# A transformer block's attention and projections written out in a fixed order on four engines

## Chip, cores and metric

One core of a Trainium2 chip runs the whole program. The time is what the device took for one execution, in microseconds. Three executions of the kernel before took 1728.81, 1731.15 and 1735.82 us; the median is 1731.15.

## What is computed

The program runs two transformer blocks on 256 tokens of 1024 features, in fp32. The change touches the first part of the first block only. Cut to that, the reference is:

```python
h = rmsnorm(x, norm1_g)
qa, ka, va, qb, kb, vb, ga, gb = split(h @ w_in)          # 1024 -> 4352
ya = neighbourhood_attention(qa, ka, va, rpb)             # 8 heads of 64, bias and window mask
qh = axial_rope(rmsnorm(qb, q_norm_g))                    # 8 heads
kh = axial_rope(rmsnorm(kb, k_norm_g))                    # 2 key/value heads, each for 4 query heads
yb = gqa_attention(qh, kh, vb)
merged = sigmoid(ga) * (ya @ w_proj_a) + sigmoid(gb) * (yb @ w_proj_b)
x = x + merged @ w_out
# then the first block's expert layer and the whole second block, which stay as they are
```

Both attentions are softmax(q k^T / 8 [+ bias and mask]) v over all 256 keys.

## The kernel before

`block1_mix` (L143) does this part. The normed input is turned to `hT`, split in two fp32r halves (hi and lo), so that a product of fp32 accuracy is three fp32r matmuls (`mm3`, L78 to L82). The input weights come as 34 blocks of 512 KB. A block is loaded by SP to a `raw` tile (four buffers), `split` (L65) makes `whi` on ScalarE (L66) and `wlo` on VectorE (L67), and there are four pairs of such tiles. With `stationary` a block is the stationary operand and 256 tokens stream: 24 matmuls of 256 columns. With `moving` a block streams past `hT`: 12 matmuls of 512 columns, or 24 of 256.

Eight blocks give the queries and keys of the first attention (`qk_block`, L175, copied to `qkT` by VectorE at L178), four its values `va`, four the queries and two the keys and values of the second attention, and sixteen the two gates (`gate`, L307, copied to `sg` by ScalarE at L310, the sigmoid later at L331). A pair of heads of the second attention goes through a norm and a rotation on VectorE (L261 to L303) before it can be scored.

`attention` (L198) does a pair of heads at a time, one head after the other:

```python
nc.tensor.matmul(pS[:, i], q_of(pair)[s, ...], k_of(pair)[s], start=True, stop=True)   # L205, 64 rows
# bias and maximum on VectorE (L212 to L218), exponential with its sum on ScalarE (L221)
# reciprocal and product on VectorE (L223, L225), four transposes (L229), copy on ScalarE (L231)
nc.tensor.matmul(pY[:, j], v_of(pair, kc), PT[j][:, kc], ...)                          # L236, 128 columns
# the head's 64 rows of pY are split into yT (hi on ScalarE, lo on VectorE)
```

The sums with V use the values of both heads as weights (128 columns) and keep the 64 rows of one. A matmul with fp32 operands (scores and sums) stands as two records in the trace; a transpose stands as one.

The order of the work is set in two ways. Where `manual_schedule` is open for an engine, its instructions stand in the order of the code. Otherwise the planner of the framework orders each engine's instructions by its own costs and priorities. Before the change only SP is in code order in `block1_mix`, and only up to the last constant (L153 to L251); TensorE, VectorE and ScalarE are the planner's. The gates are written between the pairs, two to a pair, and the planner moves them. After the gates come the four sigmoids and the products with `w_proj`, `w_out`, whose loads and splits (`load_w`, L70) the planner places too. Later parts of the program (L845, L1278) have stretches in code order on all engines.

Of the kernel before, what the change touches and what calls it, by code (L numbers as in the profile page):

```python
# [142 lines left out]
def block1_mix(e, a, x, begin):  # L143
# [7 lines left out]

    warm(e, AF.Sqrt, e.eps)
    man = tc.manual_schedule(engines={mybir.EngineType.SP})  # L153
    man.__enter__()
    for t in range(2):
        nc.sync.dma_start(x[t], a["x"][t * P:(t + 1) * P])
        if t == 0:
            g1 = row(e, pool, a["norm1_g"], D, "g1", tag="g1", eng=nc.sync)
    hT = [keep.tile([P, NC8, T], F32R, tag=f"hT{i}", name=f"hT{i}") for i in range(2)]
    for tt in range(2):  # L160
        h = wk.tile([P, D], F32, tag="h", name=f"h{tt}")
        norm_rows(e, wk, x[tt], g1, h)
        transposed(e, h, tt, hT[0], hT[1])
# [3 lines left out]
    load = wide_load(e, [(e.stage, e.raw_bufs)], [(e.stage, e.w_bufs), (pool, 2)])  # L167

    def stationary(blk, out, eng=None):
        wh, wl = load(a["w_in_a"][blk], eng=eng)  # L170
        wh, wl = (w.rearrange("p (c n) -> p c n", c=NC8) for w in (wh, wl))
        for c in range(NC8):
            mm3(e, out, wh[:, c], wl[:, c], hT[0][:, c], hT[1][:, c], c == 0, c == NC8 - 1)

    def qk_block(b):  # L175
        p = ps.tile([P, 512], F32, tag="mm", name=uid(e, "pqk"), bufs=e.mm_bufs)
        stationary(b, p[:, :T])
        nc.vector.tensor_copy(qkT[:, b], p[:, :T])  # L178

    def moving(blks, width, per):  # L180

        pt = [ps.tile([P, 512], F32, tag="mm", name=uid(e, "pmv"), bufs=e.mm_bufs) for _ in range(2)]
        for i, b in enumerate(blks):
# [12 lines left out]
    yT = [[keep.tile([P, 4, T], F32R, name=f"yT{s}{i}") for i in range(2)] for s in "ab"]  # L196

    def attention(pair, q_of, k_of, v_of, bias_of, dst):  # L198

        PT = []  # L200
        for j in range(2):
            s = slice(j * 64, (j + 1) * 64)
            pS = ps.tile([P, 2, T], F32, tag="att", name=uid(e, "pS"), bufs=e.att_bufs)
            for i, tt in enumerate((1, 0)):
                nc.tensor.matmul(pS[:, i], q_of(pair)[s, tt * P:(tt + 1) * P], k_of(pair)[s], start=True, stop=True)  # L205
            S = wk.tile([P, 2, T], F32, tag="S", name=uid(e, "S"), bufs=2)
            mx = wk.tile([P, 2], F32, tag="mx", name=uid(e, "mx"), bufs=3)
            sm = wk.tile([P, 2], F32, tag="sm", name=uid(e, "sm"), bufs=3)
            if bias_of is not None:
                b = bias_of(2 * pair + j)  # L210
# [12 lines left out]
            nc.vector.reciprocal(sm, sm)  # L223
# [20 lines left out]
    nc.sync.dma_start(bias.rearrange("p a b c -> p (a b c)"), a["na_win"])
    mask = pool.tile([P, 64], F32, name="mask")
    nc.sync.dma_start(mask, a["na_mask"])
    rope = pool.tile([P, 2, 2, 64], F32, name="rope")
    nc.sync.dma_start(rope.rearrange("p a b c -> p (a b c)"), a["rope"])
    gqk = [row(e, pool, a["gqa_q_norm_g"], 64, "gq", eng=nc.sync), row(e, pool, a["gqa_k_norm_g"], 64, "gk", eng=nc.sync)]

    man.__exit__(None, None, None)  # L251
    for b in (2, 6, 3, 7):
        qk_block(b)
    for tt, p in enumerate(moving(range(0, 4), 512, 2)):
        nc.vector.tensor_copy(va[:, tt], p)

    pq = moving(range(4, 8), 512, 2)
    pkv = moving(range(8, 10), 256, 4)
    qT = pool.tile([P, 4, T], F32, name="qT")
    kT = pool.tile([P, 2, T], F32, name="kT")  # L260
    ss = wk.tile([P, 2, 10], F32, tag="ss", name="ss", bufs=1)  # L261
    qks = []
    for tt in range(2):
        qk = wk.tile([P, 10, 64], F32, tag="qk", name=uid(e, "qk"))
        qks.append(qk)
        nc.scalar.activation(qk[:, :8].rearrange("p a b -> p (a b)"), pq[tt], AF.Copy)
        nc.scalar.activation(qk[:, 8:].rearrange("p a b -> p (a b)"), pkv[tt][:, :128], AF.Copy)
        for d in range(2):
            nc.scalar.activation(vb[:, tt, :, d], pkv[tt][:, 128:256].rearrange("p (a b) -> p a b", a=2), AF.Copy)
        sq = wk.tile([P, 10, 64], F32, tag="sq", name=uid(e, "sq"))  # L270
        nc.vector.tensor_mul(sq, qk, qk)
        nc.vector.tensor_reduce(ss[:, tt], sq, axis=AX.X, op=OP.add)
    rqk = rstd(e, wk, ss.rearrange("p a b -> p (a b)"), 20, 1.0 / 64, "gqr")
    for tt, qk in enumerate(qks):
        r = rqk[:, tt * 10:(tt + 1) * 10]
# [13 lines left out]
        nc.vector.tensor_tensor(qk, qk, rope[:, tt, 0][:, None, :].to_broadcast([P, 10, 64]), op=OP.mult)  # L289
        kd = wk.tile([P, 2, 2, 64], F32, tag="kd", name=uid(e, "kd"))  # L290
# [3 lines left out]
        qf = qk.rearrange("p h n -> p (h n)")  # L294
        kf = kd.rearrange("p a b n -> p (a b n)")
# [9 lines left out]
    sg = keep.tile([P, 16, T], F32, name="sg")  # L305

    def gate(b):  # L307
        p = ps.tile([P, 512], F32, tag="mm", name=uid(e, "pg"), bufs=e.mm_bufs)
        stationary(8 + b, p[:, :T])
        nc.scalar.activation(sg[:, b], p[:, :T], AF.Copy)  # L310

    bv = bias.rearrange("p h v c -> p h (v c)")

    def masked(h):
        if h % 2 == 0:
            v = bias[:, h:h + 2].rearrange("p a b c -> p (a b) c")
            nc.vector.tensor_tensor(v, v, mask[:, None, :].to_broadcast([P, 12, 64]), op=OP.add)
        return bv[:, h]

    for pair in range(4):  # L320
        attention(pair, lambda q: qkT[:, q], lambda q: qkT[:, 4 + q],
                  lambda q, kc: va[:, kc, q * P:(q + 1) * P], masked, yT[0])
        for b in (2 * pair, 2 * pair + 1):
            gate(b)
    for pair in range(4):
        attention(pair, lambda q: qT[:, q], lambda q: kT[:, q // 2],
                  lambda q, kc: vb[:, kc, q // 2].rearrange("p a b -> p (a b)"), None, yT[1])
        for b in (8 + 2 * pair, 9 + 2 * pair):
            gate(b)
# [1730 lines left out]
```

## Time and profile before

| what | value |
|---|---|
| median of three executions | 1731.15 us |
| profiled execution | 1730.54 us |
| its span, first to last instruction | 1728.7 us |
| mean granted TensorE clock | 0.987 |
| TensorE busy in the span | 1643.9 us (95%) |
| VectorE busy | 1117.3 us (65%) |
| ScalarE busy | 745.1 us (43%) |
| first block's part that the change touches | about 14 to 160 us |

A row of a timeline gives the start, the duration, the engine (PE is TensorE, PEld its weight loads, DVE is VectorE, ACT is ScalarE, SP issues the loads), the line of the kernel, the operation, the tile written and those read, the shape, how many instructions were merged, and in brackets how long the engine stood idle before and whose end released it. Matmuls are pipelined: the distance of two starts tells what one costs, not its duration. An instruction's busy time includes what overlaps with its neighbour.

### The profile page before, as it was taken

How to read it: one execution, taken by the hardware profiler on the slowest of the kernel's cores; microseconds unless marked ns; L12 is line 12 of the kernel's file. 1: busy time of each engine (PE TensorE's matmuls, PEld its weight loads, DVE VectorE, ACT ScalarE, POOL GpSimd, SP SyncE). 2: the span in 40 equal slices, each digit the busy share in tenths (PEclk: the TensorE clock that was granted, in tenths of full speed). 3: DMA queues.
4: the chain of work that ended last, by engine and by line, in shares of the span. 5: the costliest groups of instructions: out<-in, count | busy, mean ns of one | idle time of the engine just before them, and what ended most of it. 6: DMA issues, size and time to landing. Idle time of an engine off the chain costs nothing.

```text
span 1728.7 us, 29531 instructions
## 1 busy us (share of the span) xinstructions
PE 1643.9 (95%) x11301; PEld 1292.7 (75%) x11301; DVE 1117.3 (65%) x2212; ACT 745.1 (43%) x1217; POOL 162.2 (9%) x84
## 2 busy tenths in 40 slices
PE   7999898999999999999899998998999999999996
PEld 7888798899989999787788876987875544444442
DVE  6765789994989999877777767689653111111113
ACT  4576444444544444444454455655542222222212
POOL 0000001232112122000000003024001000000000
PEclk9999999999999999999999999999999999999998
DMA  7442744456545555587888855442067799999994
GB/s 263 145 135 62 221 157 157 155 169 191 151 131 161 170 171 172 176 287 269 300 285 286 289 162 163 146 147 76 23 266 273 273 408 409 408 409 408 409 406 159
DMA packets 108118, 390.91 MB, mean 226 GB/s; under 512 B 12656, under 2 KB 12944, under 8 KB 107840
## 3 DMA queue, kind: packets, MB, share of 16 engines
q1 hardware_dynamic: 106128, 384.58, 63.7%
q0 software_dynamic: 976, 2.82, 0.6%
q8 instruction: 91, 1.49, 0.4%
q10 hardware_dynamic: 864, 1.53, 0.3%
q14 instruction: 59, 0.48, 0.1%
HBM read 386.79 MB, written 2.10 MB: 225 GB/s over the span
## 4 chain that ended last, share of the span: by engine, by line
PE 67%; DVE 17%; DMA 9%; issue 4%; ACT 3%; POOL 0%; DVEq 0%; SPq 0%; ACTq 0%
PE pgu L1572 10%; PE acc L696 8%; DMA raw<-in_w_ada 7%; PE py L1591 5%; PE pu L80 5%; PE pu L81 5%; PE pu L82 5%; DVE wlo L67 4%; PE pga L1757 3%; PE py L1854 3%; PE pg L642 2%; PE pmv L82 1%; PE pmv L80 1%; ACT whi L66 1%; PE pmv L81 1%
## 5 line engine op out<-in xcount | busy, mean ns | idle before, releaser
L66 ACT ACTIVATE whi<-raw 128x1024 fp32r<-128x1024 f32 x361 | 379.5, 1054 | 299.0 <-PE pu L81 138.5
L67 DVE TENSOR_TENSOR wlo<-raw,whi 128x1024 fp32r<-128x1024 f32 x315 | 385.2, 1226 | 81.3 <-ACT whi L66 80.3
L82 PE MATMUL pu<-pxT,wlo 128*128 128x256 f32 x1024 | 288.7, 282 | 11.6 <-DVE wlo L67 8.8
L80 PE MATMUL pu<-pxT,whi 128*128 128x256 f32 x1024 | 290.9, 284 | 0.7 <-ACT whi L66 0.7
L81 PE MATMUL pu<-pxT,whi 128*128 128x256 f32 x1024 | 287.5, 281 | 0.0
L696 PE MATMUL acc<-whi,hh 128*128 128x512 f32 x1008 | 279.6, 395 | 6.4 <-ACT hh L66 4.2
L696 PEld LDWEIGHTS acc<-whi,hh 128*128 128x128 f32 x1008 | 189.0, 189 | 51.3 <-DVE hh L67 5.2
L82 PEld LDWEIGHTS pu<-pxT,wlo 128*128 128x128 f32 x1024 | 194.0, 189 | 14.1 <-DVE wlo L67 10.9
L80 PEld LDWEIGHTS pu<-pxT,whi 128*128 128x128 f32 x1024 | 194.0, 189 | 0.9 <-ACT whi L66 0.9
L81 PEld LDWEIGHTS pu<-pxT,whi 128*128 128x128 f32 x1024 | 194.0, 189 | 0.0
L1572 PE MATMUL pgu<-raw,xg 128*32 128x512 f32 (+2 forms) x988 | 183.4, 597 | 0.0
L67 POOL TENSOR_TENSOR wlo<-raw,whi 128x1024 fp32r<-128x1024 f32 x46 | 128.1, 2788 | 499.6 <-ACT whi L66 498.1
L696 PE MATMUL acc<-wlo,hh 128*128 128x512 f32 x504 | 157.6, 393 | 2.2 <-DVE wlo L67 2.2
L66 ACT ACTIVATE hh<-H 128x256 fp32r<-128x256 f32 x126 | 52.6, 418 | 173.4 <-PE acc L696 171.6
L1572 PEld LDWEIGHTS pgu<-raw,xg 128*32 128x32 f32 (+2 forms) x988 | 52.4, 124 | 86.5 <-issue 74.9
L696 PEld LDWEIGHTS acc<-wlo,hh 128*128 128x128 f32 x504 | 94.8, 189 | 23.7 <-DVE wlo L67 3.8
L67 DVE TENSOR_TENSOR yl<-py,yh 128x512 fp32r<-128x512 f32 x50 | 34.6, 692 | 107.1 <-ACT yh L66 107.1
L1591 PE MATMUL py<-raw,th 128*32 128x512 f32 (+2 forms) x508 | 93.7, 596 | 0.5 <-ACT th L1585 0.5
L781 DVE SCALAR_TENSOR_TENSOR ada<-raw,cs,ada 128x1024 f32<-128x1024 f32 x48 | 61.5, 1282 | 41.0 <-DMA raw<-in_w_ada 40.9
L1577 DVE SCALAR_TENSOR_TENSOR hh<-hh,sv,pgu 128x256 f32<-128x256 f32 x25 | 12.0, 479 | 117.1 <-ACT hh L1576 117.1
L1760 ACT ACTIVATE xg<-pga 128x256 f32<-128x256 f32 (+1 forms) x104 | 39.1, 376 | 110.7 <-PE pga L1757 106.6
L1757 PEld LDWEIGHTS pga<-S,hs 128*128 128x128 f32 x416 | 54.8, 189 | 36.7 <-issue 36.0
(560 smaller groups left out, 2853.7 us busy)
## 6 DMA issues: line engine op xcount, KB each, us to landing
raw<-in_w_gu SPq DMA_DIRECT2D x187, 512.0 KB, 10.1
raw<-in_peer_u SPq DMA_DIRECT2D x128, 512.0 KB, 3.6
raw<-in_peer_v SPq DMA_DIRECT2D x128, 512.0 KB, 4.5
raw<-in_w_dn SPq DMA_DIRECT2D x91, 512.0 KB, 10.1
raw<-in_w_ada SPq DMA_DIRECT2D x48, 512.0 KB, 4.7
raw<-in_w_in_a SPq DMA_DIRECT2D x24, 512.0 KB, 3.9
raw<-in_w2a SPq DMA_DIRECT2D x17, 512.0 KB, 4.2
raw<-in_w_out SPq DMA_DIRECT2D x16, 512.0 KB, 3.5
```

Of the source, the lines that this page charges most:

```text
L66: e.nc.scalar.activation(hi, src, AF.Copy)
L67: (eng or e.nc.vector).tensor_sub(lo, src, hi.bitcast(F32))
L80: nc.tensor.matmul(out, lh, rh, start=first, stop=False)
L81: nc.tensor.matmul(out, lh, rl, start=False, stop=False)
L82: nc.tensor.matmul(out, ll, rh, start=False, stop=last)
L696: nc.tensor.matmul(acc[tt][n], h[l][:, s], w[r][:, n * 512:(n + 1) * 512], start=j == order[0] and i == 0, stop=j == order[-1] and i == 2)
L781: nc.vector.scalar_tensor_tensor(mod[n], w, cs[:, c:c + 1], mod[n], op0=OP.mult, op1=OP.add)
L1572: nc.tensor.matmul(pg[t], xx[:, c, t], ws[i][:, k * 512:(k + 1) * 512], start=c == 0, stop=c == NC8 - 1)
L1591: nc.tensor.matmul(py[q][t], th[:, k, t], w[i][:, q * 512:(q + 1) * 512], start=k == 0, stop=last and k == 1)
L1757: nc.tensor.matmul(p[:, :n].rearrange("p u n -> p (u n)"), hs[i][:, tt, q * P:(q + 1) * P], S[:, tt, :n].rearrange("p u n -> p (u n)"), st ...
L1760: nc.scalar.activation(xg[:, q, :n], p[:, :n], AF.Copy)
L1854: nc.tensor.matmul(acc[tt][n], St[:, tt * P:(tt + 1) * P], y[:, n * 512:(n + 1) * 512], start=first and v == 0 and w == 0, stop=v == len(u ...
```

## The change

All of `block1_mix` up to the last gate is put in code order on SP, TensorE, VectorE and ScalarE, and the code is rearranged. The 34 blocks stand in one list; a block's use splits the block two ahead and loads up to five ahead. `attention` becomes three functions: `scores` (scores, bias, maximum and exponential of both heads, the heads' matmuls alternating), `weights` (normalising, transposes, copies), `sums` (with 64-column weights, the heads alternating, into the two halves of one PSUM tile, one split for both). The rotation becomes `squares`, `roots`, `scaled`, `rotated`, `added`, `placed`, called between products. Four buffers of S and of its maxima and sums, where there were two and three. The products, the bytes and the shapes of all else stay.

```diff
+    man = tc.manual_schedule(engines={SP, PE, DVE, Activation})      # names cut
+    man.__enter__()
     warm(e, AF.Sqrt, e.eps)
-    man = tc.manual_schedule(engines={mybir.EngineType.SP})
-    man.__enter__()
...
+    seq = [("w_in_a", b) for b in (0, 4, 1, 5)] + [("w_in_b", b) for b in (4, 5, 6, 7, 8, 9, 0, 1, 2, 3)]
+    seq += [("w_in_a", b) for b in (2, 6, 3, 7, *range(8, 24))]
+    def fetch(n):
+        while len(raws) < min(n, len(seq)):
+            nm, b = seq[len(raws)]
+            raws.append(load_raw(e, a[nm][b]))
+    def cut(n):
+        while len(pairs) < min(n, len(seq)):
+            k = len(pairs)
+            fetch(k + 1)
+            where, bufs = ((e.stage, e.w_bufs), (pool, 2))[k % 2]
+            w = [where.tile([P, 1024], F32R, tag=g, name=uid(e, g), bufs=bufs) for g in ("whi", "wlo")]
+            split(e, *w, raws[k])
+            pairs.append(w)
+    def block():
+        used[0] += 1
+        cut(used[0] + 2)
+        fetch(used[0] + 5)
+        return pairs[used[0] - 1]
...
+    def scores(n):
+        q, k, _, b0, _ = (near + far)[n]
+        pSs = [ps.tile([P, 2, T], F32, tag="att", name=uid(e, "pS"), bufs=e.att_bufs) for _ in heads]
+        for i, tt in enumerate((1, 0)):
+            for s, pS in zip(heads, pSs):
+                nc.tensor.matmul(pS[:, i], q[s, tt * P:(tt + 1) * P], k[s], start=True, stop=True)
+        if b0 is not None:
+            v = bias[:, b0:b0 + 2].rearrange("p a b c -> p (a b) c")
+            nc.vector.tensor_tensor(v, v, mask[:, None, :].to_broadcast([P, 12, 64]), op=OP.add)
+        out = []
+        for j, pS in enumerate(pSs):
...      # S, mx, sm (four buffers each), bias or scale, maximum, exponential: as before
+            out.append((S, sm))
+        going[n] = out
+    def weights(n):
+        for S, sm in going[n]:
             nc.vector.reciprocal(sm, sm)
             for i in range(2):
                 nc.vector.tensor_scalar(S[:, i], S[:, i], sm[:, i:i + 1], None, op0=OP.mult)
...      # four transposes, copy to PT: as before
-        pY = ps.tile([P, 2, T], F32, tag="att", name=uid(e, "pY"), bufs=e.att_bufs)
-        for j in range(2):
-            for kc in range(2):
-                nc.tensor.matmul(pY[:, j], v_of(pair, kc), PT[j][:, kc], start=kc == 0, stop=kc == 1)
-        for j in range(2):
-            s = slice(j * 64, (j + 1) * 64)
-            split(e, dst[0][s, pair], dst[1][s, pair], pY[s, j])
+    def sums(n):
+        v_of, dst = (near + far)[n][2], (near + far)[n][4]
+        pY = ps.tile([P, 512], F32, tag="mm", name=uid(e, "pY"), bufs=e.mm_bufs)[:, :T]
+        for kc in range(2):
+            for s, pt in zip(heads, going[n]):
+                nc.tensor.matmul(pY[s], v_of(kc)[:, s], pt[:, kc], start=kc == 0, stop=kc == 1)
+        split(e, *dst, pY)
...
+    qk_block(0)
+    qk_block(4)
+    scores(0)
+    qk_block(1)
+    qk_block(5)
+    scores(1)
+    pq = moving(4, 512, 2)
...      # queries of the second attention to qks on ScalarE
+    pkv = moving(2, 256, 4)
...      # keys to qks and values to vb on ScalarE
+    pv = moving(4, 512, 2, (partial(squares, 0), partial(squares, 1), roots))   # one piece behind each block
+    weights(0)
+    for tt in range(2):
+        nc.vector.tensor_copy(va[:, tt], pv[tt])
+    qk_block(2)
+    scaled(0)
+    weights(1)
+    sums(0)
+    qk_block(6)
+    rotated(0)
+    scores(2)
+    sums(1)
+    qk_block(3)
+    added(0)
+    qk_block(7)
+    placed(0)
+    scaled(1)
+    scores(3)
+    weights(2)
+    gate()
+    rotated(1)
+    sums(2)
+    gate()
+    weights(3)
+    added(1)
+    gate()
+    placed(1)
+    sums(3)
+    scores(4)
+    gate(2)
+    for n in range(4, 8):
+        if n < 7:
+            scores(n + 1)
+        weights(n)
+        gate(3 if n == 7 else 2)
+        sums(n)
+    gate(2)
+    man.__exit__(None, None, None)
     for b in (0, 8, 4, 12):
         nc.scalar.activation(sg[:, b:b + 4], sg[:, b:b + 4], AF.Sigmoid)
```

`scaled` is L276 to L278 of the kernel before, `rotated` L285 and L289, `added` L292 and L293, `placed` the transposes and copies L298 to L303.

## Rows read from the trace of the kernel before

**Rows 1.** Stretches of the first block: length, PE, PEld, DVE, ACT, POOL busy, clock, DMA.
```profile
66.75:87.20 20.45, 18.66 (x149) 17.48 (x148) 20.38 (x53) 13.83 (x28) 0.00 (x0) 1.00 0.27 81
...
124.00:157.40 33.40, 33.39 (x195) 26.01 (x193) 17.92 (x49) 21.64 (x57) 0.00 (x0) 1.00 0.12 36
```
**Rows 2.** Waits of TensorE, 60 to 160 us (total, times, longest).
```profile
PE pqT L298 <- DVE qk L293: 1.7, 2, 1.2
```
**Rows 3.** Timeline, 0 to 60 us, two matmuls of one block.
```profile
22.33 0.28 PE L81 MATMUL pqk<-hT,whi 128*128 128x256 f32 x1
...
22.45 0.28 PE L82 MATMUL pqk<-hT,wlo 128*128 128x256 f32 x1
```
**Rows 4.** Timeline of TensorE, 128 to 158 us, one head's turn.
```profile
133.54 1.13 PE L236 MATMUL pY<-PT,vb 128*128 128x256 f32 x4
134.60 1.13 PE L205 MATMUL pS<-kT,qT 64*128 64x256 f32 x4
135.66 0.66 PE L229 MATMUL pT<-ident,S 128*128 128x128 f32 x4
136.07 0.36 PE L82 MATMUL pg<-hT,wlo 128*128 128x256 f32 x1
```
**Rows 5.** Timeline, 60 to 90 us, the scores of pair 0.
```profile
66.75 1.14 PE L205 MATMUL pS<-qkT 64*128 64x256 f32 x8
```
**Rows 6.** TensorE's groups by shape, 1400 to 1440 us (busy, mean ns).
```profile
L1572 PE MATMUL pgu<-raw,xg 128*128 128x512 f32 x16 | 7.5, 599 | 0.0
L1572 PE MATMUL pgu<-raw,xg 128*64 128x512 f32 x16 | 3.9, 605 | 0.0
```
**Rows 7.** Timeline of VectorE, 1055 to 1075 us.
```profile
1069.36 0.69 DVE L130 TENSOR_TENSOR mhT<-ptr,mhT 128x512 fp32r<-128x512 f32 x1 [1.34 <-ACT mhT L129]
...
1071.52 0.15 DVE L864 TENSOR_TENSOR mss<-mss 128x2 f32<-128x2 f32 x1
```
**Rows 8.** Timeline of ScalarE, 1062 to 1073 us.
```profile
1068.65 0.18 ACT L861 ACTIVATION_READ_ACCUMULATOR mh<-xg 128x1 f32 x1
```
**Rows 9.** Groups by shape, 0 to 250 us (busy, mean ns, idle before).
```profile
L67 DVE TENSOR_TENSOR wlo<-raw,whi 128x1024 fp32r<-128x1024 f32 x62 | 75.1, 1220 | 30.5 <-ACT whi L66 29.9
L66 ACT ACTIVATE whi<-raw 128x1024 fp32r<-128x1024 f32 x64 | 67.2, 1058 | 68.6 <-PE pq L81 15.5 <-PE pmv L82 13.1 <-PE pqk L81 12.1
...
L225 DVE TENSOR_SCALAR S<-S,sm 128x256 f32<-128x256 f32 x32 | 10.0, 350 | 0.4
...
L221 ACT ACTIVATE S<-S,mx 128x256 f32<-128x256 f32 x16 | 8.0, 499 | 1.5 <-DVE mx L214 1.5
...
L212 DVE SCALAR_TENSOR_TENSOR S<-pS,bias 128x256 f32<-128x256 f32 x16 | 6.2, 417 | 1.7 <-PE pS L205 1.6
...
L217 DVE TENSOR_REDUCE mx<-pS 128x2 f32<-128x512 f32 x8 | 5.5, 692 | 3.6 <-PE pS L205 3.6
...
L214 DVE TENSOR_REDUCE mx<-S 128x2 f32<-128x512 f32 x8 | 5.4, 680 | 0.1
...
L221 ACT ACT_TABLE_LOAD x4 | 5.1, 1283 | 0.3 <-DVE mx L218 0.3
...
L317 DVE TENSOR_TENSOR bias<-bias,mask 128x768 f32<-128x768 f32 x4 | 3.6, 950 | 0.0
L178 DVE COPY qkT<-pqk 128x256 f32<-128x256 f32 x8 | 3.4, 425 | 4.9 <-PE pqk L82 4.9
...
L271 DVE TENSOR_TENSOR sq<-qk 128x640 f32<-128x640 f32 x2 | 1.6, 822 | 0.5 <-ACT qk L267 0.5
```
**Rows 10.** VectorE's busy time on the tiles qk, 66.75 to 88.5 us.
```profile
66.75:88.50 21.75, 9.98 (x20) 1.00 0.27 79
```
**Rows 11.** The same for what reads the sines and cosines.
```profile
66.75:88.50 21.75, 3.41 (x6) 1.00 0.27 79
```
**Rows 12.** Busy time by engine and granted clock (after POOL's column) around 211.8 us.
```profile
206.10:211.80 5.70, 1.83 (x8) 1.15 (x8) 4.37 (x8) 2.56 (x5) 0.00 (x0) 1.00 0.48 131
213.50:216.00 2.50, 2.50 (x13) 2.49 (x13) 0.99 (x2) 0.60 (x1) 1.67 (x2) 0.50 0.76 241
```

More of the change, by code (lines that the diff above doesn't have):

```diff
@@ L150, in block1_mix @@
     ps = e.ps
+    man = tc.manual_schedule(engines={mybir.EngineType.SP, mybir.EngineType.PE, mybir.EngineType.DVE, mybir.EngineType.Activation})
+    man.__enter__()
     warm(e, AF.Sqrt, e.eps)
-    man = tc.manual_schedule(engines={mybir.EngineType.SP})
-    man.__enter__()
     for t in range(2):
@@ L158, in block1_mix @@
             g1 = row(e, pool, a["norm1_g"], D, "g1", tag="g1", eng=nc.sync)
+    seq = [("w_in_a", b) for b in (0, 4, 1, 5)] + [("w_in_b", b) for b in (4, 5, 6, 7, 8, 9, 0, 1, 2, 3)]
+    seq += [("w_in_a", b) for b in (2, 6, 3, 7, *range(8, 24))]
+    raws, pairs, used = [], [], [0]
+    def fetch(n):
[10 more added lines that the diff above has]
+            pairs.append(w)
@@ new lines, in block @@
+    def block():
[3 more added lines that the diff above has]
+        return pairs[used[0] - 1]
+    fetch(4)
+    bias = pool.tile([P, 8, 6, 64], F32, name="bias")
+    nc.sync.dma_start(bias.rearrange("p a b c -> p (a b c)"), a["na_win"])
+    mask = pool.tile([P, 64], F32, name="mask")
+    nc.sync.dma_start(mask, a["na_mask"])
+    rope = pool.tile([P, 2, 2, 64], F32, name="rope")
+    nc.sync.dma_start(rope.rearrange("p a b c -> p (a b c)"), a["rope"])
+    gqk = [row(e, pool, a["gqa_q_norm_g"], 64, "gq", eng=nc.sync), row(e, pool, a["gqa_k_norm_g"], 64, "gk", eng=nc.sync)]
@@ L159, in block1_mix @@
     hT = [keep.tile([P, NC8, T], F32R, tag=f"hT{i}", name=f"hT{i}") for i in range(2)]
+    h = [wk.tile([P, D], F32, tag="h", name=f"h{tt}") for tt in range(2)]
     for tt in range(2):
-        h = wk.tile([P, D], F32, tag="h", name=f"h{tt}")
-        norm_rows(e, wk, x[tt], g1, h)
-        transposed(e, h, tt, hT[0], hT[1])
-    qkT = pool.tile([P, 8, T], F32, name="qkT")
[L167 to L171, printed above, removed]
+        norm_rows(e, wk, x[tt], g1, h[tt])
@@ L172, in stationary @@
+    for tt in range(2):
+        cut(tt + 1)
+        transposed(e, h[tt], tt, hT[0], hT[1])
+    def stationary(out):
+        wh, wl = (w.rearrange("p (c n) -> p c n", c=NC8) for w in block())
         for c in range(NC8):
             mm3(e, out, wh[:, c], wl[:, c], hT[0][:, c], hT[1][:, c], c == 0, c == NC8 - 1)
+    qkT = pool.tile([P, 8, T], F32, name="qkT")
     def qk_block(b):
         p = ps.tile([P, 512], F32, tag="mm", name=uid(e, "pqk"), bufs=e.mm_bufs)
-        stationary(b, p[:, :T])
+        stationary(p[:, :T])
@@ L178, in qk_block, with moving @@
         nc.vector.tensor_copy(qkT[:, b], p[:, :T])
-    def moving(blks, width, per):
+    def moving(n, width, per, between=()):
         pt = [ps.tile([P, 512], F32, tag="mm", name=uid(e, "pmv"), bufs=e.mm_bufs) for _ in range(2)]
-        for i, b in enumerate(blks):
-            wh, wl = load(a["w_in_b"][b])
-            wh, wl = (w.rearrange("p (c n) -> p c n", c=per) for w in (wh, wl))
+        for i in range(n):
+            wh, wl = (w.rearrange("p (c n) -> p c n", c=per) for w in block())
@@ L191, in moving @@
                         c == 0, c == NC8 - 1)
+            for f in between[i:i + 1]:
+                f()
         return pt
@@ L196, in block1_mix @@
     yT = [[keep.tile([P, 4, T], F32R, name=f"yT{s}{i}") for i in range(2)] for s in "ab"]
-    def attention(pair, q_of, k_of, v_of, bias_of, dst):
-        PT = []
-        for j in range(2):
-            s = slice(j * 64, (j + 1) * 64)
[L203 to L210, printed above, removed]
+    qT = pool.tile([P, 4, T], F32, name="qT")
+    kT = pool.tile([P, 2, T], F32, name="kT")
+    bv = bias.rearrange("p h v c -> p h (v c)")
+    heads = [slice(j * 64, (j + 1) * 64) for j in range(2)]
+    near = [(qkT[:, q], qkT[:, 4 + q], lambda kc, q=q: va[:, kc, q * P:(q + 1) * P], 2 * q, [t[:, q] for t in yT[0]])
+            for q in range(4)]
+    far = [(qT[:, q], kT[:, q // 2], lambda kc, q=q: vb[:, kc, q // 2].rearrange("p a b -> p (a b)"), None,
+            [t[:, q] for t in yT[1]]) for q in range(4)]
+    going = {}
+    def scores(n):
[9 more added lines that the diff above has]
+        for j, pS in enumerate(pSs):
+            S = wk.tile([P, 2, T], F32, tag="S", name=uid(e, "S"), bufs=4)
+            mx = wk.tile([P, 2], F32, tag="mx", name=uid(e, "mx"), bufs=4)
+            sm = wk.tile([P, 2], F32, tag="sm", name=uid(e, "sm"), bufs=4)
+            if b0 is not None:
+                b = bv[:, b0 + j]
                 for i in range(2):
@@ L244, in block1_mix @@
[L244 to L260, printed above, removed]
-    ss = wk.tile([P, 2, 10], F32, tag="ss", name="ss", bufs=1)
[L262 to L271, printed above, removed]
+        going[n] = PT
@@ new lines, in sums @@
+    def sums(n):
[5 more added lines that the diff above has]
+        split(e, *dst, pY)
+    ss = wk.tile([P, 2, 10], F32, tag="ss", name="ss", bufs=1)
+    qks = [wk.tile([P, 10, 64], F32, tag="qk", name=uid(e, "qk")) for _ in range(2)]
@@ L272, in block1_mix, with squares, roots @@
+    ros = [wk.tile([P, 10, 64], F32, tag="ro", name=uid(e, "ro")) for _ in range(2)]
+    def squares(tt):
+        sq = wk.tile([P, 10, 64], F32, tag="sq", name=uid(e, "sq"), bufs=1)
+        nc.vector.tensor_mul(sq, qks[tt], qks[tt])
         nc.vector.tensor_reduce(ss[:, tt], sq, axis=AX.X, op=OP.add)
-    rqk = rstd(e, wk, ss.rearrange("p a b -> p (a b)"), 20, 1.0 / 64, "gqr")
-    for tt, qk in enumerate(qks):
-        r = rqk[:, tt * 10:(tt + 1) * 10]
+    def roots():
+        going["r"] = rstd(e, wk, ss.rearrange("p a b -> p (a b)"), 20, 1.0 / 64, "gqr")
@@ L276, in block1_mix, with scaled @@
+    def scaled(tt):
+        qk, r = qks[tt], going["r"][:, tt * 10:(tt + 1) * 10]
         nc.vector.tensor_tensor(qk, qk, r[:, :, None].to_broadcast([P, 10, 64]), op=OP.mult)
@@ L278, in block1_mix, with rotated @@
         nc.vector.tensor_tensor(qk[:, 8:], qk[:, 8:], gqk[1][:, None, :].to_broadcast([P, 2, 64]), op=OP.mult)
+    def rotated(tt):
+        qk, ro = qks[tt], ros[tt]
         q4 = qk.rearrange("p h (s f n) -> p (h s) f n", s=2, f=2)
-        ro = wk.tile([P, 10, 64], F32, tag="ro", name=uid(e, "ro"))
         r4 = ro.rearrange("p h (s f n) -> p (h s) f n", s=2, f=2)
@@ L289, in block1_mix, with added @@
         nc.vector.tensor_tensor(qk, qk, rope[:, tt, 0][:, None, :].to_broadcast([P, 10, 64]), op=OP.mult)
+    def added(tt):
+        qk, ro = qks[tt], ros[tt]
         kd = wk.tile([P, 2, 2, 64], F32, tag="kd", name=uid(e, "kd"))
@@ L293, in block1_mix, with placed @@
         nc.vector.tensor_add(qk[:, :8], qk[:, :8], ro[:, :8])
-        qf = qk.rearrange("p h n -> p (h n)")
-        kf = kd.rearrange("p a b n -> p (a b n)")
+        going["k", tt] = kd
+    def placed(tt):
+        qf = qks[tt].rearrange("p h n -> p (h n)")
+        kf = going["k", tt].rearrange("p a b n -> p (a b n)")
         p = ps.tile([P, 4, P], F32, tag="tr", name=uid(e, "pqT"), bufs=e.tr_bufs)
@@ L305, in block1_mix @@
     sg = keep.tile([P, 16, T], F32, name="sg")
[L307 to L329, printed above, removed]
+    gates = iter(range(16))
@@ new lines, in gate @@
+    def gate(n=1):
+        for _ in range(n):
+            b = next(gates)
+            p = ps.tile([P, 512], F32, tag="mm", name=uid(e, "pg"), bufs=e.mm_bufs)
+            stationary(p[:, :T])
+            nc.scalar.activation(sg[:, b], p[:, :T], AF.Copy)
+    qk_block(0)
[5 more added lines that the diff above has]
+    pq = moving(4, 512, 2)
+    for tt in range(2):
+        nc.scalar.activation(qks[tt][:, :8].rearrange("p a b -> p (a b)"), pq[tt], AF.Copy)
@@ new lines, in block1_mix @@
+    pkv = moving(2, 256, 4)
+    for tt in range(2):
+        nc.scalar.activation(qks[tt][:, 8:].rearrange("p a b -> p (a b)"), pkv[tt][:, :128], AF.Copy)
+        for d in range(2):
+            nc.scalar.activation(vb[:, tt, :, d], pkv[tt][:, 128:256].rearrange("p (a b) -> p a b", a=2), AF.Copy)
+    pv = moving(4, 512, 2, (partial(squares, 0), partial(squares, 1), roots))
+    weights(0)
+    for tt in range(2):
+        nc.vector.tensor_copy(va[:, tt], pv[tt])
+    qk_block(2)
+    scaled(0)
```

6 lines of the change are left out of this document (1 added, 5 removed).

## Prediction

> **What bounds the kernel now.** I read the slices of the page first, for the clock and the load of each engine, then the busy time of three stretches of the first block, then TensorE's instructions one after another, and last VectorE's and ScalarE's durations by shape. The first block's products and attention run from 14.3 us to about 160 us. In the last third of it TensorE is busy 33.39 of 33.40 us and VectorE 17.92; only in the 20 us around the rotation does VectorE take over (20.38 of 20.45) and TensorE stands a little [rows 1]: both waits for the rotated queries come to 1.7 us [rows 2]. Matmuls of 256 columns start 0.12 us apart [rows 3], so a block of 24 costs 2.88 us on TensorE. The 34 blocks fill most of the stretch and are the same after the change. So the kernel gains what the change takes off TensorE, and loses each time that TensorE, now bound to a written order, stands before an instruction whose operand is late.
>
> **What TensorE is spared.** The scores of one head (four recorded matmuls) hold it 1.06 us: pS at 134.60, the next instruction at 135.66 [rows 4]. For pair 0 both heads' scores stand side by side: eight take 1.14 us [rows 5], for the heads sit on different rows of the array. The change writes all eight pairs that way: seven gain 2 x 1.06 - 1.14 = 0.98, together 6.9 us. The sums P·V cost 1.06 us a head as well (133.54 to 134.60 [rows 4]); the change cuts their weights to 64 columns and alternates the heads. That form with these operands is not in the stretch, but later 16 matmuls of 128\*64 take 3.9 us where 16 of 128\*128 take 7.5 [rows 6], so eight should cost 1.1 instead of 2.12: 8 x 1.02 = 8.2 us. The bounds are 0 (no overlap) and 8.5. The 1.7 us of waits and some 0.9 at the block's end, where the last yTb was late, go too. Sum: **-17.7 us**. Fewer splits of yT (16 to 8 on each engine) and six table loads saved on ScalarE lie beside TensorE's work: nothing.
>
> The page "TensorEngine Tiling (Array Packing)" of the Trainium skill (Key Properties) says that a change of tiling mode drains the engine, which speaks against narrow products spread over the block. The sums get a mode of their own, so 16 more changes; by the 0.1 us by which the first full matmul after a group is longer (0.36 against 0.28 [rows 3, 4]) that would add 1.6 us. In [rows 4] it stands behind full-width transposes, where no mode changes, so it is no price of the mode and I leave it out of the sum.
>
> **What the order adds.** Does a fixed order hold? In a later stretch that is already written out, VectorE turns a tile (L130 at 1069.36 after 1.34 us of idling) and reaches the sum L864 at 1071.52 [rows 7], whose operand ScalarE had finished at 1068.83 [rows 8]. It was ready 0.5 us before L130 and waited 2.7 us, behind what stands before it in the code. So I walk the new text engine by engine with the durations of [rows 9]. The prices: copy of a block to qkT 0.43; a near pair's scores on VectorE 0.95 for the mask, then twice (2 x 0.42 + 0.68) = 3.0; a far pair's two maxima with their scaling some 1.65; the normalising of one head a small reciprocal of 0.15 [rows 7] and 2 x 0.35, a little overlapped, 0.78; a split 1.06 on ScalarE, then 1.22 on VectorE; the exponentials 1.0 a head. The rotation's pieces: all work on qk takes 9.98 us for both tiles [rows 10], less the two squares of 0.82, that is 4.2 a tile; the products with sine and cosine are 3.41 / 2 = 1.7 of it [rows 11]; the rest, 2.5, splits by columns (1280 to 768) into 1.55 for `scaled` and 0.95 for `added`.
>
> (a) scores(0) and scores(2) stand right behind the block whose copy they read: drain 0.16 (0.28 against 0.12 [rows 3]) + 0.43, twice: 1.2.
> (b) scores(1). Behind pair 0's scores VectorE works 1.5 on the first head, ScalarE loads the table (1.28) and does both heads (2.0), then whi 1.06, wlo 1.22, copy 0.43, wlo 1.22, copy 0.43: 9.1. TensorE has two blocks, 5.8. Less small overlaps: 3.1.
> (c) transposes of pair 0. From pkv's end ScalarE copies 1.0 and splits 1.06; VectorE then has four wlo 4.9, squares and their sums 4 x 0.82, thirteen small root instructions at 0.15 [rows 7], normalising 0.8: 13.0. TensorE has pv, 48 matmuls of 512 columns at a little under twice 0.12, 10.8: 2.2.
> (d) transposes of pair 1: copy of block 2 (0.6 with drain), `scaled`(0) 1.55, normalising 0.78, all in front: 2.9.
> (e) the deepest one. From pair 2's scores to pair 2's transposes VectorE's queue is: rest of `rotated` 0.4, mask 0.95, scores 3.0, waiting for exponentials and yT's hi 1.4, lo 0.4, waiting for whi and wlo 1.85, copy 0.43, `added` 0.95, wlo 1.22, copy 0.43, two copies of the placed tile 1.1, `scaled`(1) 1.55, pair 3's mask and scores 3.95, normalising 0.78: 18.4, less overlaps 17.8. TensorE has sums, two blocks, six transposes and scores, 8.9: it stands 8.9 in three pieces, about 6 of it before pair 2's transposes.
> (f) transposes of pair 3, behind yT's lo and a split: 0.7.
> (g) pairs 4 to 6. The code calls scores(n+1) and then weights(n), so VectorE's maxima of n+1, which wait for the scores just issued, come before the normalising of n, and TensorE's next instruction is n's transposes: 1.65 + 0.78 + 0.1 = 2.5, three times: 7.5. Behind it wait two gate products that need nothing.
> (h) pair 7: yT's split 0.8 before its normalising 0.78: 1.7.
> (i) the second head's normalising against four transposes of 0.4 to 0.6 [rows 4]: 0.25 x 7 = 1.8.
> (j) the end. ScalarE and VectorE come to the first w_proj split only behind the last gate's copy: 0.4 + 1.06 + 1.22, 2.8. Bounds: 0.3, if the split may go ahead; 8.5, if four sigmoids of about a whi's time and two table loads go first.
> (k) the clock. Before 211.8 us TensorE has 1.83 us of work in 5.70; after it the granted clock is 0.50 (1.2 GHz) for at least 2.5 us [rows 12], which loses 1.25. The gap in (e) is as long: 1.3. The other gaps are shorter; bounds 0 and 5.
>
> The loads move too: SP issues all 34 in one list, four in flight, two blocks split ahead. TensorE passes a block each 2.9 us or slower and the tensors w_proj are behind the last of them as now. Nothing.
>
> Added: 1.2 + 3.1 + 2.2 + 2.9 + 8.9 + 0.7 + 7.5 + 1.7 + 1.8 + 2.8 + 1.3 = **34.1 us**. Net 34.1 - 17.7 = 16.4. What follows the block has the same work and only starts later. The profiled execution took 1730.5 us, 0.6 under the median of 1731.15 (span 1728.7). 1730.5 + 16.4 = 1747; as overlaps were taken off only roughly, I say **1746 us**.
>
> The page "TensorE: Matmul & The Clock Gate" of the Trainium skill (Architectural detail) calls VectorE and ScalarE strict first-in-first-out queues, and lets TensorE pull only weight loads ahead, not matmuls. By it the waits stand as counted; if engines could pass a waiting instruction, (e) to (i) would shrink to almost nothing. [rows 7, 8] agree with the page.
>
> **Rivals.**
> *TensorE's saving wins.* The stalls (b) to (e) count on VectorE being late each time. If ScalarE and VectorE run far enough ahead there, only (a), (g), (h) and half of (j) remain, some 12, or less where the order does not bind: 1730.5 - 17.7 + 1 to 12, about 1713 to 1725. It decides from where all stalls sum to less than 17.7. For it: VectorE has only 17.92 us of work in the last 33.4 [rows 1]. Against it: its idle time lies behind waits, not ahead of them, and (e) is pure queue length.
> *Even.* Half of the stalls are covered by TensorE's own lateness: 17 added, 17.7 gone, 1730.
> *The heads do not overlap.* Alternating weight loads of different tiles serialise: scores and sums stay at 2.1 a pair, 1746 + 15 = 1761. Against it [rows 5, 6].
> *The end is worse.* The sigmoids go before the first split: + 5.7, 1752.
>
> **Chances.** A measurement of this kernel tells about 0.5%, 8.7 us, from no change. Forecast with the worse end 0.70 (1739 to 1755), heads not overlapping 0.04, even 0.13, saving wins 0.13. So slower 0.74, within 0.13, faster 0.13. The likeliest case's own range is 1739 to 1755; down to 1725 it takes in the even case and the edge of the saving.
>
> **What would show it.** Scores and sums with eight matmuls in 1.1 us each; TensorE waiting for VectorE's normalising (L225's successor) before the transposes, about 2.5 us at three places and some 6 us once near 90 us; waits of TensorE for the rotation's copies small; gates' last product at about 172 us against 157 now. If TensorE waits less than 10 us in all in the block, the forecast is wrong at (b) to (e); if the sums take 2 us, at the saving.

## The result, and the profile after

The changed kernel takes 1752.48 us (median of five executions, 1746.23 to 1753.35); the kernel before took 1735.46 beside it (five executions, 1728.81 to 1735.82). The ratio is 1.0106, 95% interval 1.0076 to 1.0135: 18 us more, with 13 to 23 inside the interval; the two medians alone differ by 17.0. The profiled execution after has a span of 1750.6 us and a mean granted clock of 0.978; before it was 1728.7 and 0.987.

The place to read the loss is the start of the products with `w_proj`, the first work behind the changed stretch. Here are those products (tile pp) on TensorE, per line: duration as min/median/max in ns, then first and last start.

```profile
L80 PE MATMUL pp<-yTa,whi x32: 283/283/283, 178.3 to 198.1; 128*128 128x256 f32 x32
```

They run 192 in a row, 0.12 us apart, that is 23.0 us. In the kernel before they are mixed with the last pair's sums:

```profile
L80 PE MATMUL pp<-yTa,whi x32: 279/283/468, 157.5 to 180.5; 128*128 128x256 f32 x32
...
L82 PE MATMUL pp<-yTb,wlo x32: 279/283/283, 162.3 to 183.6; 128*128 128x256 f32 x32
```

The last ended at about 183.7, so 23.0 us of them would have begun at 160.7. The stretch became 178.3 - 160.7 = **17.6 us longer**, about what the medians differ by. The two profiled spans differ by 21.9 us; the other 4.3 lie behind the stretch, where the instructions are the same. That part took 1568.0 us before, 1572.3 after, and 1569.6 to 1574.8 in the traces of four runs further down, so no reading here rests on it. Three views of the kernel after say where it came from. First, what TensorE waited for between 14 and 200 us (total, times, longest), where before there were 1.7 us [rows 2] and 0.9 at the end:

```profile
PE pT L286 <- DVE S L282: 18.9, 8, 5.8
PE pS L251 <- DVE qkT L214: 3.8, 4, 2.1
PE pqT L345 <- DVE qk L337: 2.3, 1, 2.3
```

Together 25.0 us, every one for VectorE. Second, TensorE's timeline at several places:

```profile
90.58 0.66 PE L345 MATMUL pqT<-ident,qk 128*128 128x128 f32 x4 [2.34 <-DVE qk L337]
...
92.06 1.13 PE L251 MATMUL pS<-qkT 64*128 64x256 f32 x8 [0.60 <-DVE qkT L214]
99.03 1.94 PE L286 MATMUL pT<-ident,S 128*128 128x128 f32 x8 [5.84 <-DVE S L282]
...
100.98 0.41 PE L81 MATMUL pg<-hT,whi 128*128 128x256 f32 x1
101.19 0.41 PE L82 MATMUL pg<-hT,wlo 128*128 128x256 f32 x1
...
115.24 1.13 PE L251 MATMUL pS<-kT,qT 64*128 64x256 f32 x8
116.31 0.39 PE L80 MATMUL pg<-hT,whi 128*128 128x256 f32 x1
...
122.25 1.13 PE L251 MATMUL pS<-kT,qT 64*128 64x256 f32 x8
125.71 1.44 PE L286 MATMUL pT<-ident,S 128*128 128x128 f32 x8 [2.33 <-DVE S L282]
126.91 0.36 PE L80 MATMUL pg<-hT,whi 128*128 128x256 f32 x1
...
132.84 1.08 PE L297 MATMUL pY<-PT,vb 128*64 128x256 f32 x8
133.85 1.13 PE L251 MATMUL pS<-kT,qT 64*128 64x256 f32 x8
```

By the distance of starts, eight scores hold TensorE 1.07 us (115.24 to 116.31) and eight sums 1.01 (132.84 to 133.85), against 1.06 for half as many [rows 4]. The three waits 2.34, 0.60 and 5.84 are pair 2's queue, the 2.33 before a far pair's transposes is the pattern of the last loop. Behind the 5.84 the gate's products start 0.21 us apart, where [rows 3] has 0.12. Third, therefore, the clock in six stretches (length, then PE, PEld, DVE, ACT, POOL busy, then the granted clock, DMA share, GB/s):

```profile
32.10:35.30 3.20, 3.20 (x11) 2.18 (x12) 1.87 (x4) 0.00 (x0) 0.00 (x0) 0.50 0.83 252
66.10:69.40 3.30, 3.30 (x18) 3.30 (x17) 1.51 (x2) 1.26 (x2) 0.00 (x0) 0.50 0.11 46
73.00:76.30 3.30, 3.30 (x16) 2.08 (x16) 0.68 (x3) 1.19 (x2) 0.00 (x0) 0.50 0.00 0
99.00:103.60 4.60, 4.57 (x22) 4.57 (x23) 1.80 (x5) 2.69 (x6) 0.00 (x0) 0.50 0.00 0
137.90:141.10 3.20, 3.20 (x17) 3.08 (x16) 0.62 (x2) 2.17 (x4) 0.00 (x0) 0.50 0.00 0
151.50:154.80 3.30, 3.30 (x18) 3.30 (x17) 0.72 (x1) 2.55 (x7) 0.00 (x0) 0.50 0.01 2
...
sum 20.90, PE 20.87 PEld 18.51 DVE 7.19 ACT 9.86 POOL 0.00; mean PE 3.48 PEld 3.08 DVE 1.20 ACT 1.64 POOL 0.00
```

TensorE works 20.87 us at 0.50, the lower level of 1.2 GHz. At 0.21 us for what costs 0.12 at the upper one, it loses some 20.87 x (1 - 0.12 / 0.21) = 9 us.

### The profile page after: what moved, and what is told of

The parts are those of the page before. It is cut to its first block, busy times and chain, and to the rows that moved or that the text cites. A ratio compares the mean times of both kernels' runs of the same rounds, so it can differ in the third digit from the quotient of the medians.

```text
span 1750.6 us, 29521 instructions
## 1 busy us (share of the span) xinstructions
PE 1644.4 (94%) x11301; PEld 1291.8 (74%) x11301; DVE 1114.2 (64%) x2204; ACT 738.4 (42%) x1207; POOL 161.3 (9%) x84
## 3 DMA queue, kind: packets, MB, share of 16 engines
q8 instruction: 91, 1.49, 0.4%
## 4 chain that ended last, share of the span: by engine, by line
PE 68%; DVE 18%; DMA 7%; issue 3%; ACT 3%; POOL 0%; DVEq 0%; SPq 0%; ACTq 0%
PE pgu L1656 10%; PE acc L780 9%; PE pu L80 5%; PE pu L82 5%; PE pu L81 5%; PE py L1675 5%; DMA raw<-in_w_ada 5%; DVE wlo L67 4%; PE pga L1841 3%; PE py L1938 3%; PE pg L726 2%; ACT whi L66 1%; PE pmv L80 1%; PE pmv L82 1%; PE pmv L81 1%
## 5 line engine op out<-in xcount | busy, mean ns | idle before, releaser
L80 PEld LDWEIGHTS pu<-pxT,whi 128*128 128x128 f32 x1024 | 196.5, 192 | 0.9 <-ACT whi L66 0.9
L81 PEld LDWEIGHTS pu<-pxT,whi 128*128 128x128 f32 x1024 | 196.7, 192 | 0.0
```

Source lines behind the costliest of these rows:

```text
L80: nc.tensor.matmul(out, lh, rh, start=first, stop=False)
L81: nc.tensor.matmul(out, lh, rl, start=False, stop=False)
```

## The experiments

Beside each group of runs the kernel before was measured on the same chip (medians 1731.4, 1733.9 and 1733.3), and the ratios are to it. Theory: the written order makes TensorE wait, and the waits cost clock besides. Rivals: the new form of scores and sums costs something by itself; the clock costs next to nothing; only the place of one call is bad.

**The order taken away.** The new text stays; of the four engines only SP keeps the order of the code, as before.

```diff
-    man = tc.manual_schedule(engines={SP, PE, DVE, Activation})
+    man = tc.manual_schedule(engines={SP})
```

> The changed text with only SP in code order; TensorE, VectorE and ScalarE go back to the planner. Theory (the order costs, the new forms pay): TensorE's 25 us of waits shrink to a few, no half-clock stretch, 5 to 15 us under the kernel before. Rival (the new forms or the fixed list of blocks cost the time): 10 us or more over the kernel before, whoever orders.

Measured: 1710.86 us (1708.01 to 1716.19), ratio 0.9867 [0.982, 0.9913]: by the medians 21 us under before and 42 under the kernel after, which was measured at another time. It is faster than both. Windows and pp of this run:

```profile
14.00:60.00 46.00, 46.00 (x286) 40.73 (x285) 40.43 (x73) 25.06 (x44) 0.00 (x0) 1.00 0.65 212
60.00:100.00 40.00, 40.00 (x320) 34.96 (x319) 33.92 (x74) 24.50 (x52) 0.00 (x0) 1.00 0.40 122
100.00:140.00 40.00, 40.00 (x330) 36.60 (x329) 20.29 (x41) 29.60 (x61) 0.00 (x0) 1.00 0.43 133
...
L80 PE MATMUL pp<-yTa,whi x32: 283/283/283, 139.6 to 159.4; 128*128 128x256 f32 x32
```

TensorE never stands, the clock is 1.00, and pp starts 38.7 us before that of the kernel after with the same instructions of the stretch. So the loss is the order. The new text as a whole is worth 21.1 us: that much earlier than the 160.7 of before does pp start. Added up from the distances of TensorE's starts in the two traces, scores and sums hold it some 14 us less, its waits are 2.8 less, and most of the rest lies in the gates' products, which hold it 47.5 us instead of 50.7; why these fell was not traced. (The profiled execution, the slowest of the four, has a span only 14.3 us under before: behind the stretch it took 6.8 more.)

**The gaps filled.** The text after, with 158 products of 256 columns whose result is overwritten, put before the instructions that wait.

```diff
+    fill = {0: 10, 1: 19, 2: 44, 4: 15, 5: 15, 6: 15, 7: 9}
...
             pT = ps.tile([P, 2, T], F32, tag="tr", ...)
+            for _ in range(fill.get(n, 0) if j == 0 else 0):
+                nc.tensor.matmul(pT[:, 0], hT[0][:, 0, :P], hT[0][:, 0], start=True, stop=True)
...      # and 15 before pair 1's scores, 16 before the first rotated queries
```

> The changed kernel with 158 useless products of 256 columns (hT by hT, into the tile that the transposes or scores then overwrite) in the gaps where TensorE waits: 10, 19, 44, 15, 15, 15, 9 before the transposes of pairs 0, 1, 2, 4, 5, 6, 7, 16 before the first rotated queries, 15 before pair 1's scores. Results the same; TensorE does about 19 us more. Theory (the half clock behind the gaps costs about 10 us): the half-clock stretches go and the kernel is 7 to 10 us faster than the changed one, some 8 to 10 over the kernel before. Rival (the waits are all): as the changed kernel, 17 over, or a little more.

Measured: 1743.36 us (1737.15 to 1747.27), ratio 1.0063 [1.0043, 1.0083]: 9 us under the kernel after by the medians, 7 by the two ratios, with 158 x 0.12 = 19 us more of work on TensorE. Five windows:

```profile
14.00:60.00 46.00, 44.62 (x267) 39.00 (x266) 29.36 (x44) 22.24 (x41) 0.00 (x0) 1.00 0.54 178
...
60.00:75.00 15.00, 14.19 (x103) 12.03 (x102) 10.89 (x30) 4.67 (x7) 0.00 (x0) 1.00 0.34 106
75.00:100.00 25.00, 23.18 (x182) 20.41 (x182) 19.82 (x41) 9.03 (x23) 0.00 (x0) 1.00 0.21 64
100.00:125.00 25.00, 24.55 (x192) 21.45 (x189) 15.83 (x35) 16.88 (x37) 0.00 (x0) 1.00 0.34 106
125.00:150.00 25.00, 24.49 (x191) 21.22 (x190) 12.92 (x28) 16.50 (x35) 0.00 (x0) 1.00 0.31 90
```

The clock does not fall in any of them, and pp starts at 170.0 instead of 178.3, 8.3 us earlier. About half of the 17.6 us was the clock.

**A gate ahead of the normalising, far loop.**

```diff
             scores(n + 1)
+        gate()
         weights(n)
-        gate(3 if n == 7 else 2)
+        gate(2 if n == 7 else 1)
```

> The changed kernel with one gate product put between scores(n+1) and weights(n) in the loop over pairs 4 to 7 (one gate before weights, the rest behind). Theory: there TensorE waits 7.0 us for the normalising that stands behind the next pair's maxima, and two half-clock stretches of 3.4 us follow these waits; both go: 7.0 + about 3.4 less, so the kernel stands 6 to 8 us over the kernel before instead of about 17. If the clock is no part of it, about 10 over. Rival (the wait only moves, for VectorE is full): about 17 over, with the 7 us of waits now in front of another instruction.

Measured: 1753.74 us (1753.02 to 1755.6), ratio 1.0122 [1.0076, 1.0168]: no gain. The wait before pair 4's transposes grew from 2.33 to 3.97, and VectorE's timeline shows why:

```profile
120.84 0.17 DVE L269 TENSOR_SCALAR mx<-mx 128x2 f32<-128x2 f32 x1
124.49 1.23 DVE L67 TENSOR_TENSOR wlo<-raw,whi 128x1024 fp32r<-128x1024 f32 x1 [3.48 <-ACT whi L66]
125.63 0.16 DVE L280 RECIPROCAL sm<-sm 128x2 f32<-128x2 f32 x1
```

A gate brings its split with it. The split's hi part stands on ScalarE behind a table load and four exponentials of the next pair (120.29 to 123.4), VectorE stands 3.48 us for it, and the normalising of a pair whose exponentials were long done stands behind that. The rival, that the wait only moves, held.

**The normalising itself moved.** `weights` is cut in `norm` and `turn`, and in the far loop `norm(n + 1)` comes behind the first gate, ahead of `sums(n)`.

```diff
+    norm(4)
     for n in range(4, 8):
         if n < 7:
             scores(n + 1)
-        weights(n)
-        gate(3 if n == 7 else 2)
+        turn(n)
+        gate()
+        if n < 7:
+            norm(n + 1)
         sums(n)
+        gate(2 if n == 7 else 1)
```

> The changed kernel with one edit in the loop over pairs 4 to 7: the normalising of pair n+1 stands behind a gate, before the sums of n, so ahead of the maxima of n+2 and not behind a weight split that waits for ScalarE, as it did with the gate put in between. All else as in the changed kernel. Theory: three waits of 2.3 us, the one of 1.5 and two half-clock stretches of about 1.7 us each go: 10 to 12 us under the changed kernel, so 5 to 8 over the kernel before. Rival (as with the gate: the wait goes elsewhere): 17 to 22 over.

Measured: 1740.9 us (1736.71 to 1744.67), ratio 1.0034 [1.0013, 1.0055], where the kernel after has 1.0106. Waits from 110 to 170 us fall from 8.5 us to this one line, and the mean clock of 125 to 175 us is 1.00, where it was 0.93:

```profile
PE pY L300 <- ACT PT L291: 2.1, 2, 1.2
```

By the two ratios that is 12 of the 18 us, and pp starts at 167.4, 10.9 us earlier than in the kernel after: most of the loss sat in the order of the last loop's lines.

**The whole order written anew.** `norm` ahead of the next pair's maxima from pair 1 on, scores a block or more behind the copy that they read, `placed` one or two gates behind `added`, one gate block earlier in the list; all four engines in code order.

```diff
-    weights(0)
...
+    norm(1)
     qk_block(2)
+    turn(0)
     scaled(0)
-    weights(1)
-    sums(0)
     qk_block(6)
+    turn(1)
+    sums(0)
+    gate()
-    rotated(0)
     scores(2)
     sums(1)
...
```

> The changed kernel, all four engines still in code order, but in another order: weights is cut in norm (VectorE) and turn (transposes, copies); norm of a pair always stands a block or more ahead of its turn and ahead of the next pair's maxima, scores stand a block behind the copies that they read, placed behind two gates. Same instructions. Theory (the places of the waits cost, not that the order is fixed): TensorE waits under 6 us, and the kernel is about where the planner's order of the same text is, 15 to 22 us under the kernel before. Rival (a fixed order of four engines cannot follow ScalarE and VectorE): waits of over 15 us remain, at or over the kernel before.

Measured: 1729.22 us (1724.66 to 1734.35), ratio 0.9973 [0.9953, 0.9993]: 5 us under before, though not the planner's 21. No stretch has a lower clock than 1.00 up to pp, which starts at 153.1. The two largest waits left before it:

```profile
PE pY L300 <- ACT PT L291: 4.3, 3, 1.6
PE pT L289 <- DVE S L281: 1.9, 2, 1.6
...
```

A fixed order as such need not lose; this one had waits in it. With three smaller ones (1.1, 0.5 and 0.4) they make 8.2 of the 13.5 us by which pp is behind the planner's 139.6; the rest was not traced.

**The forms alone, in the text before.** Five kernels with the planner's order: the narrow sums alone, or both heads' scores and sums, with 2 or 4 buffers of S, and pY in a buffer of the products (tag mm) or of the scores (att). A tag names a group of buffers that its tiles take in turn.

```diff
-        pY = ps.tile([P, 2, T], F32, tag="att", ...)
+        pY = ps.tile([P, 512], F32, tag="mm", ...)[:, :T]      # or tag="att"
-        for j in range(2):
-            for kc in range(2):
-                nc.tensor.matmul(pY[:, j], v_of(pair, kc), PT[j][:, kc], ...)
+        for kc in range(2):
+            for s, pt in zip(heads, PT):
+                nc.tensor.matmul(pY[s], v_of(pair, kc)[:, s], pt[:, kc], ...)
...      # one split of pY; the alternating scores and the buffers of S are not shown
```

Both forms (alternating scores and narrow sums), two buffers of S, tag mm:

> The kernel before with one thing of the change: the scores and the sums of both heads of a pair alternate, sums with 64-column weights, one split of yT for both. Order by the planner as before. Theory: TensorE bounds the stretch and is spared 15.1 us, of which some is lost to later maxima: 8 to 15 us under the kernel before. Rival (TensorE is not the bound there, or the narrow forms do not overlap): within 3 us of it.

Measured 1765.54 us (1760.15 to 1768.33), ratio 1.0193 [1.0146, 1.024], 34 us over before: the theory missed. Both forms, four buffers, tag mm:

> The kernel before with alternating scores and sums as already tried, but with four buffers each of S, its maxima and its sums in place of two and three. Theory A (two S buffers made the next pair's scores wait): at least 15 us faster than with two, so 15 over the kernel before or less. Theory B (the planner has nothing to put between, as a pair is one call and the rotation one lump): as with two buffers, 25 to 35 over.

Measured 1746.32 us (1737.77 to 1753.21), ratio 1.0075 [1.0053, 1.0096]: the buffers were some 20 us of it, not all. Narrow sums alone, tag mm:

> The kernel before with the narrow sums alone: 64-column weights, heads alternating, pY in a buffer of the products, one split of yT for both heads; scores head by head as before, planner's order. Theory: TensorE is spared 8 us and its stretch stays full: 5 to 9 us under the kernel before. Rival (any look of the planner's order hangs on the details): off by 10 us or more either way.

Measured 1762.12 us (1760.94 to 1762.23), ratio 1.0148 [1.0118, 1.0179]: missed as well. Its timeline of TensorE at the rotation:

```profile
72.14 1.76 PE L205 MATMUL pS<-qkT 64*128 64x256 f32 x4 [0.46 <-DVE S L212]
81.88 1.09 PE L297 MATMUL pqT<-ident,qk 128*128 128x128 f32 x4 [7.98 <-DVE qk L292]
...
89.83 0.39 PE L80 MATMUL pg<-hT,whi 128*128 128x256 f32 x1
```

No gate product lies in the rotation; the first comes at 89.8, where before has 67.8. The gates stand behind pair 0 in the text, and pY now takes its turn in their buffers. The last two runs test that:

> The kernel before with 64-column sums alone (both heads alternating, one split), as in the run in which pY had moved to the four buffers of the products and which took 28 us more than before; here pY stays in the buffers of the scores. Theory A (the buffer did it: in that run TensorE stood 8.0 us for the rotation at 73.9 to 81.9 us and the first gate product came at 89.8 us, where before has it at 67.8, because a gate written behind pair 0's sums takes its buffer of products only after pY has one): gates start near 68 us again, no wait of 8 us, and 8.2 us less of TensorE's work shows: 1723 to 1728, 5 to 9 us under before. Theory B (the narrow sums themselves cost, by changes of the array's form or by the planner's costs): the time stays 10 to 28 us over before.

> The kernel before with both heads' scores and the 64-column sums alternating and four buffers of S, mx, sm, the planner's order, and pY in the two buffers of the scores (the same with pY in a buffer of products took 12 us more than before). Theory A (the products' buffer held the gates back): the gates lie under the rotation again, 15 us less of TensorE's work shows in part or in whole: 1714 to 1722. Theory B (a pair's two pS take both buffers of the scores, pY needs one of the same two, so the next pair's scores wait until the sums are split, and the planner cannot look ahead): gates under the rotation, but TensorE waits before scores or sums in every pair: 1725 to 1745.

Measured: narrow sums with tag att 1741.18 us (1736.38 to 1744.57), ratio 1.0041 [1.0025, 1.0058]; both forms with tag att 1738.47 us (1732.98 to 1741.74), ratio 1.0031 [1.0017, 1.0045]. The buffer was right: the gates start at 68.1 and 67.1, the 8 us wait is gone, and by the medians 21 and 8 us with it. The times promised by theory A were not reached, by 13 us and more. Both forms with tag att came into theory B's range, but not for its reason: TensorE did not wait before scores there, and before sums only 0.7 us in all. The gates of the narrow sums' run, and the end of its stretch, show what is bound there instead (TensorE, then ScalarE in the next fence):

```profile
L80 PE MATMUL pg<-hT,whi x128: 274/283/388, 68.1 to 151.7; 128*128 128x256 f32 x128
...
160.11 0.66 PE L229 MATMUL pT<-ident,S 128*128 128x128 f32 x4
...
161.45 0.65 PE L237 MATMUL pY<-PT,vb 128*64 128x256 f32 x2 [0.45 <-ACT PT L231]
164.38 0.81 PE L229 MATMUL pT<-ident,S 128*128 128x128 f32 x4 [2.28 <-DVE S L225]
...
165.87 1.54 PE L237 MATMUL pY<-PT,vb 128*64 128x256 f32 x5 [0.45 <-ACT PT L231]
```

```profile
153.55 1.28 ACT L330 ACT_TABLE_LOAD   x1
...
156.41 1.28 ACT L221 ACT_TABLE_LOAD   x1
...
159.02 1.28 ACT L116 ACT_TABLE_LOAD   x1
...
161.42 1.28 ACT L221 ACT_TABLE_LOAD   x1
```

The last gate product starts at 151.9 (before: 157.4). Then the last pair's heads go through one after the other with only a few products of pp beside them, and four table loads, 5.1 us, for the sigmoid, the root and the exponentials in turn, stand around their exponentials; before, the sigmoid's and the root's loads came at 159.5 and 162.2, behind the last exponential. The last sums of the last pair start at 165.87, where the kernel before has them earlier:

```profile
159.28 0.92 PE L236 MATMUL pY<-PT,vb 128*128 128x256 f32 x3
```

From these traces it seems that in the old text the saved work only uncovers the chain of the attention. In the new text the planner issues pair 0's scores at 22.4 us instead of 66.8 [rows 5], and then the gates last to the end. That the early scores are what does it is inferred from these traces; no run changed them alone.

## Why the prediction was right, and where it was not

Direction and size came out: 16 us more were forecast and 17 to 18 came, for the reason given. That the sum came so close is in part luck: the clock cost some 7.7 us more than forecast, and the end, the waits and the saving erred the other way by 2.8, 3.2 and 1.1.

- **What TensorE is spared:** -17.7. The forecast set durations of eight (1.14 and 1.1) against the distance of starts for four (1.06). By starts, eight scores hold TensorE 1.07 and eight sums 1.01, so the two forms are worth 7 x 1.05 + 8 x 1.11 = 16.2 instead of 15.1, the sums a little more than their upper bound of 8.5. The planner's run shows that a gain of this size is real (pp 21.1 us earlier).
- **Waits (a) to (h):** 28.2 forecast, 25.0 measured, all for VectorE as said. By place, forecast/measured: (a) 1.2/1.04; (b) 3.1/2.15; (c) 2.2/1.71; (d) 2.9/2.73; (e) 8.9/8.78 (2.34 + 0.60 + 5.84); (f) 0.7/0.18; (g) 7.5/6.97; (h) 1.7/1.49. (The terms written out for (h) and (j) add up to 1.6 and 2.7, a tenth less than was put in.) Adding up a fixed order's queue from durations of the trace came within 1 us at every place, and mostly within half of one. [rows 7, 8] had it right: no instruction is seen to pass a waiting one.
- **(i) second heads:** eight transposes held TensorE 1.20 us at 125.71 (to 126.91); where both heads were ready, at 88.46 in the run of the narrow sums with tag att, they held it 0.79. Forecast 0.25 a pair, measured 0.4 there and at four other pairs, so some 3 us for 1.8.
- **(j) the end:** 2.8 forecast, 0 measured. The step assumed that ScalarE and VectorE come to the first split of `w_proj` only behind the last gate's copy. They came to it before:

```profile
168.43 1.06 ACT L415 ACTIVATE sg<-sg 128x1024 f32<-128x1024 f32 x1
169.39 0.36 ACT L360 ACTIVATE sg<-pg 128x256 f32<-128x256 f32 x1
169.66 1.99 ACT L66 ACTIVATE whi<-raw 128x1024 fp32r<-128x1024 f32 x2
171.55 0.38 ACT L360 ACTIVATE sg<-pg 128x256 f32<-128x256 f32 x1
```

  Line 415 is the sigmoid behind the stretch; it stands between two gate copies of the stretch. Code order binds the instructions in the stretch to each other, and those outside may be put between them.
- **(k) the clock:** 1.3 forecast with bounds of 0 and 5, about 9 measured, by the half-clock stretches and again by the filled gaps. The step that was mis-sized is "The other gaps are shorter": one row of a long gap [rows 12] was taken to mean that shorter ones are free. The clock fell behind gaps of 2.15, 1.71, 2.73, 5.84 and two of 2.3 us.

Sum of what was measured: - 16.2 - 2.6 + 25.0 + some 3 + 9 = 18, where 17.6 was read. The last gate's product came at 178.2, not about 172, by the clock above all. The rival of the saving failed as its own condition says, with waits above 17.7; "the heads do not overlap" failed by 1.07 and 1.01; "the end is worse" failed with (j).

## What to carry over

Before an order is written by hand, walk each engine's queue and ask of every instruction what it makes the next one wait for; put finished work (here the normalising) ahead of work that has yet to wait, on every engine, and remember that a call brings its loads and splits with it. Price new gaps of TensorE twice, once as waiting and once for the clock behind them: here 25.0 us of waits brought some 9 us at the lower clock. And try the rearranged text with the planner's order first: here the rearrangement was worth 20 us, and the order took away 40.

## What had not been expected of the hardware

After gaps of 1.7 to 5.8 us the granted clock was 0.50 for 3.2 to 4.6 us of work. It was not so after every gap: 2.33 us before 125.71 had no drop behind it, 2.32 before 137.30 had one, from some 0.5 us after the work began again:

```profile
125.70:129.00 3.30, 3.28 (x25) 2.96 (x26) 0.82 (x4) 3.30 (x11) 0.00 (x0) 1.00 0.12 45
137.30:141.10 3.80, 3.80 (x19) 3.51 (x20) 1.19 (x5) 2.77 (x7) 0.00 (x0) 0.56 0.00 0
```

What tells the two apart stays open. Products of no use in the gaps, 19 us of them, made the kernel 7 to 9 us faster.
